# Linear-attention output gates: projected and applied in the gate stages instead of the GLA heads

## The chip, the cores and the metric

The kernel runs on one core of a Trainium2 chip. The metric is device time in microseconds (us), the median of several runs. The engines are TensorE (PE in the profile, with its weight loads as PEld), VectorE (DVE), ScalarE (ACT), GpSimd (POOL) and SyncE (SP), which here issues transfers only. ScalarE issues transfers as well, beside its own work.

## What is computed

One layer of a hybrid decoder over 2048 tokens of width 1024, with 16 extra tokens ahead. All is in float32. From u = RMSNorm(h), one combined projection gives the inputs of two branches (a Mamba-2 SSD branch and a gated linear attention branch, GLA) and the merge gates:

```python
z, xbc, dt_raw, q, k, v, g_gla, a_lr, merge_g = split_cols(proj, IN_WIDTHS)
...
o = rmsnorm(jnp.concatenate([o_m, o_r], axis=1), gla_norm_w)
y_gla = o.reshape(b, l, GLA_DV) * jax.nn.silu(g_gla)
branches = jnp.stack([y_ssd.astype(y_gla.dtype), y_gla], axis=2)
branch_proj = jnp.einsum('blnc,ncd->blnd', branches, w_branch)
gates = jax.nn.sigmoid(merge_g.reshape(b, l, N_BRANCH, D_MODEL))
merged = jnp.sum(gates * branch_proj, axis=2)
return hres + jnp.einsum('bld,de->ble', merged, w_out)
```

The change is about `g_gla`, the output gate of the linear attention (4 heads of 256 columns), and the product `o * silu(g_gla)`. The result then gets a last RMSNorm.

## The kernel before

**Precision.** Every large product is made of three matmuls: both factors are split into a high part (a rounded copy) and a low part (the rest), and high x high, high x low and low x high are summed (`accum`, L186 to L190). A split is one ScalarE copy and one VectorE or POOL subtraction.

**First stage.** Four blocks of 512 tokens (block 0 with the 16 extra tokens). In a block come 4 SSD units (`ssd_proj`) and 4 GLA heads (`gla_proj`, L625). A feature tile (`proj_feat`, L192) is a projection onto 128 columns: 8 x 3 = 24 matmuls of 512 columns, in two halves by weight transfer. A token-side projection (`proj_tok`, L204) of v is 96 matmuls of 256 columns. A GLA head projects q, k, v, and two feature tiles of the output gate; for each of these ScalarE makes tanh (L654) and VectorE (1 + tanh) times the value (L655), which is twice the silu. Weights are split in block 0, kept in memory (`k_...`), and reloaded by SP in blocks 1 to 3 (`load_w`, L164).

**Scans.** The recurrent part of a unit is a Python generator (`ssd_scan`, `gla_scan`), cut into segments by `yield`. `begin` starts one; each `yield` of a projection calls `step`, which runs one segment of every generator that is alive. So the segments stand between the projection's matmuls in TensorE's program, which is executed in the order written, as is SP's (`manual_schedule`). The order on VectorE, ScalarE and POOL is chosen by the scheduler when the kernel is built; each engine then works through its own list in order. A GLA scan has 11 segments: levels of the causal product (`level_in` on VectorE and ScalarE, L704 to L712; `level_out` on TensorE, L719), diagonal sums (L783), a merged matrix (L785 to L791), its transposes (L798), four chunks that accumulate output and state (L805 to L816: L809 on TensorE reads the state that L810 on VectorE writes for the chunk before), a normalization, transposes (L824), the gate's product on VectorE (L825), and the stores of y (L828). Beside these, `fetch_u` makes the next block's u (L248, L254), and `beside_unit` makes sums of u or y that the second stage needs (L80 on POOL).

**Second stage.** Gate stage, branch 0 and branch 1 for each of two superblocks of 1024 tokens, then the output stage (L1048). A stage is made of units. A unit takes 2 x 2 blocks of products (two feature tiles, two token blocks) in seven products instead of eight (Strassen's scheme in Winograd's form), 12 matmuls of 512 columns each, 84 in all, where single products would take 96. Units go in pairs. Each product is a step (`product`, L950); what else is issued at a step is set by a table of positions (`todo`, L1065): weight loads 7.5 steps ahead (`load_a`, four transfers and four POOL sums, L937 to L940), splits 5 steps ahead (`prep_a`, L946 and L947), the next stage's operand from 12 steps ahead (`prep_b`, L922 and L923). A gate stage has 8 units; `use` (L978) applies tanh to each of a unit's four results and stores it. Branch stages fetch these and p (L991) and multiply (L1002). Sums that are not ready in the first stage are made from `spots` (L1084).

## Time and profile before

| What | us |
| --- | --- |
| median of 3 runs | 2337.64 (2336.07 to 2343.33) |
| the profiled execution, whole | 2350.0 |
| its span from first to last instruction | 2348.2 |
| first stage with its last scan's end | 0 to 1554.4 |
| the GLA parts of blocks 0 to 3 in it | 196.4, 223.0, 226.7, 212.1 |
| second stage | 1554.4 to the end |

The profile lists busy times of each engine, groups of equal instructions by line and operands (count, busy time, mean duration, and the idle time just before them with what ended it), and single instructions in order of time. The durations of TensorE's instructions overlap, since they are pipelined, so their spacing or their busy time together is read, not one duration. "Idle before" is time in which that engine had nothing to run; on TensorE it is a wait that the kernel pays for, elsewhere it may cost nothing. The granted clock is the share of full speed that TensorE was given.

### The profile page before, as it was taken

Reading aid. Unit: us, or ns where it says so; the run is one execution under the profiler, and the core shown is the slowest. Engines: PE = TensorE matmul, PEld = TensorE weight load, DVE = VectorE, ACT = ScalarE, POOL = GpSimd, SP = SyncE. Lnnn points to the kernel's source line nnn. Section 1 sums busy time; section 2 is a strip of 40 time slices with the busy share of each in tenths; the row PEclk is TensorE's granted clock in tenths of the full one; section 3 lists DMA queues with packets and bytes.
Section 4 is the critical chain, followed back from the end, with each engine's and each line's share of the span. In section 5 each row is a group of like instructions: output and inputs, shape, how many; then the busy total and the mean of one; then the engine's idle time right before and its main releaser. Section 6 shows DMA issues by size and latency. Waiting matters only on the chain.

```text
span 2348.2 us, 36518 instructions
## 1 busy us (share of the span) xinstructions
PE 2253.1 (96%) x12651; PEld 1966.1 (84%) x12651; DVE 1566.5 (67%) x2884; ACT 1188.2 (51%) x2764; POOL 684.1 (29%) x677
## 2 busy tenths in 40 slices
PE   6899999999999999999999999889999999999998
PEld 6889989888888989798988898768788788777886
DVE  4676666676665667576568555674578864788876
ACT  5666655465534455543466443464555454544543
POOL 2344533122321212211122200207433355422441
PEclk9999999999999999999999999889999999999999
DMA  7665875767786666776676655447668866778762
GB/s 240 225 201 198 296 242 193 223 200 229 255 266 202 200 225 214 247 251 214 192 231 218 205 166 164 146 157 240 212 225 283 274 226 211 261 243 275 232 198 108
DMA packets 300937, 515.89 MB, mean 220 GB/s; under 512 B 27616, under 2 KB 143584, under 8 KB 300752
## 3 DMA queue, kind: packets, MB, share of 16 engines
q1 hardware_dynamic: 200080, 401.17, 52.9%
q10 hardware_dynamic: 100672, 112.39, 13.8%
q8 instruction: 99, 1.62, 0.3%
q14 instruction: 86, 0.70, 0.1%
HBM read 366.26 MB, written 147.19 MB: 219 GB/s over the span
## 4 chain that ended last, share of the span: by engine, by line
PE 39%; DMA 5%; DVE 4%; issue 2%; ACT 2%; SPq 0%; POOL 0%; ACTq 0%; DVEq 0%; POOLq 0%
PE psa L188 5%; PE psa L190 4%; PE psa L189 4%; PE pj L188 4%; PE pj L190 4%; PE pj L189 4%; PE psb L188 2%; PE psb L189 2%; PE psb L190 2%; DMA br<-br_t 2%; PE psc L188 1%; PE psc L189 1%; PE psc L190 1%; DMA br<-gate_t 1%; DVE b L923 1%
## 5 line engine op out<-in xcount | busy, mean ns | idle before, releaser
L188 PE MATMUL pj<-u,whl 128*128 128x512 f32 (+1 forms) x1184 | 450.6, 381 | 17.3 <-ACT acc L495 9.0
L190 PE MATMUL pj<-u,whl 128*128 128x512 f32 (+1 forms) x1184 | 433.9, 366 | 0.4 <-POOL whl L176 0.4
L189 PE MATMUL pj<-u,whl 128*128 128x512 f32 (+1 forms) x1184 | 433.5, 366 | 0.0
L188 PE MATMUL pj<-whl,u 128*128 128x256 f32 (+1 forms) x992 | 289.9, 292 | 2.7 <-ACT u L249 1.8
L190 PE MATMUL pj<-whl,u 128*128 128x256 f32 (+1 forms) x992 | 283.0, 285 | 3.9 <-DVE u L254 3.9
L189 PE MATMUL pj<-whl,u 128*128 128x256 f32 (+1 forms) x992 | 282.9, 285 | 0.7 <-POOL whl L176 0.7
L188 PEld LDWEIGHTS pj<-u,whl 128*128 128x128 f32 x1184 | 227.8, 192 | 56.7 <-ACT acc L495 10.0
L188 PE MATMUL psa<-b,a 128*128 128x512 f32 x640 | 253.1, 395 | 15.1 <-ACT sn L963 13.1
L190 PEld LDWEIGHTS pj<-u,whl 128*128 128x128 f32 x1184 | 227.0, 192 | 36.5 <-POOL whl L176 0.6
L189 PEld LDWEIGHTS pj<-u,whl 128*128 128x128 f32 x1184 | 227.9, 192 | 33.5
L190 PE MATMUL psa<-b,a 128*128 128x512 f32 x640 | 251.6, 393 | 0.0
L189 PE MATMUL psa<-b,a 128*128 128x512 f32 x640 | 251.5, 393 | 0.0
L947 DVE TENSOR_TENSOR a<-ar,a 128x512 fp32r<-128x512 f32 x160 | 151.6, 955 | 75.0 <-ACT a L946 73.2
L188 PEld LDWEIGHTS pj<-whl,u 128*128 128x128 f32 x992 | 190.5, 192 | 4.3 <-ACT u L249 1.9
L190 PEld LDWEIGHTS pj<-whl,u 128*128 128x128 f32 x992 | 190.4, 192 | 4.2 <-DVE u L254 4.2
L176 POOL TENSOR_TENSOR whl<-wr,whl 128x512 fp32r<-128x512 f32 (+1 forms) x100 | 135.3, 1360 | 199.3 <-ACT whl L175 155.8
L80 POOL TENSOR_TENSOR wr<-wr 128x256 f32<-128x256 f32 x80 | 66.9, 836 | 433.2 <-DMA wr<-y 178.2
L189 PEld LDWEIGHTS pj<-whl,u 128*128 128x128 f32 x992 | 190.5, 192 | 1.4 <-POOL whl L176 0.9
L923 DVE TENSOR_TENSOR b<-br,b 128x512 fp32r<-128x512 f32 x196 | 149.1, 783 | 48.4 <-ACT b L922 47.5
L937 POOL TENSOR_TENSOR as<-ar,ar 128x512 f32<-128x512 f32 x40 | 60.2, 1505 | 414.5 <-DMA ar<-in_w_br 107.8
L499 DVE SCALAR_TENSOR_TENSOR acc<-cin,hcw,acc 128x512 f32<-128x512 f32 (+1 forms) x192 | 154.8, 806 | 32.4 <-ACT acc L495 31.1
L922 ACT ACTIVATE b<-br 128x512 fp32r<-128x512 f32 x196 | 119.5, 626 | 95.7 <-DMA br<-br_t 36.6
(278 smaller groups left out, 5073.2 us busy)
## 6 DMA issues: line engine op xcount, KB each, us to landing
whl<-k_s SPq DMA_DIRECT2D x96, 512.0 KB, 4.2
whl<-k_g SPq DMA_DIRECT2D x96, 512.0 KB, 4.2
whl<-k_v SPq DMA_DIRECT2D x48, 512.0 KB, 3.8
whl<-k_z SPq DMA_DIRECT2D x36, 512.0 KB, 3.8
wr<-in_w_feat SPq DMA_DIRECT2D x64, 256.0 KB, 4.4
k_s<-whl SPq DMA_DIRECT2D x32, 512.0 KB, 3.9
cb<-cumd ACTq DMA_DIRECT2D x64, 256.0 KB, 5.6
y<-gg ACTq DMA_DIRECT2D x64, 256.0 KB, 4.4
```

What stands on the lines that cost most here:

```text
L80: nc.gpsimd.tensor_tensor(o, x, y, op=ALU.subtract)
L176: nc.gpsimd.tensor_tensor(hl[:, 1], raw, hl[:, 0].bitcast(F32), op=ALU.subtract)
L188: nc.tensor.matmul(ps, sh, mh, start=first, stop=False, **kw)
L189: nc.tensor.matmul(ps, sh, ml, start=False, stop=False, **kw)
L190: nc.tensor.matmul(ps, sl, mh, start=False, stop=last, **kw)
L499: nc.vector.scalar_tensor_tensor(acc, cin[:, k:k + tt], hcw[:, ti, k:k + 1], acc, op0=ALU.mult, op1=ALU.add)
L922: nc.scalar.activation(t[:, 0], raw, AF.Copy)
L923: nc.vector.tensor_tensor(t[:, 1], raw, t[:, 0].bitcast(F32), op=ALU.subtract)
L937: nc.gpsimd.tensor_tensor(s1, a21, a22, op=ALU.add)
L947: nc.vector.tensor_tensor(t[:, 1], src, t[:, 0].bitcast(F32), op=ALU.subtract)
```

## The change

The two gate tiles of each head leave `gla_proj`. A scan now stores the normalized y without its gate (L825 becomes a ScalarE activation, L826 of the changed file). A gate stage has 12 units instead of 8: the first eight alternate between a GLA head's gate and a merge gate. For a GLA unit it fetches y two products ahead, multiplies it with the projection, then with 1 + tanh, and stores the gated y under a new name (`yg`). Sums for branch 1 read `yg`, so those of the first superblock can't be made in block 2 any more: they move to the end of gate stage 0, and those of the second to the end of gate stage 1.

The projections of q, k and v of GLA heads yield at half pieces with a value of 0.5. `step` now counts: a generator of rate 1 runs a segment every two half steps, a GLA scan (rate 1.5) three in four; SSD units step as before. The scan begins before the last yield of v. Its old segments 10 and 11 are one. Buffers for y in the first stage (`gg`) go from 4 to 3.

```diff
-        yield from proj_tok(f"v{h}", w_tok[SG + h], o.u, o.starts + [0] * o.ci0, places)
+        yield from proj_tok(f"v{h}", w_tok[SG + h], o.u, o.starts + [0] * o.ci0, places, part=HALF)
...
-        yield
-        gs = []
-        for j in range(2):
-            ps, = proj_feat(f"g{t0 + 2 + j}", w_feat[t0 + 2 + j], o.segs_real, o.mov)
-            gg = mk(wk, [P, BLK], F32, "gg", bufs=4)
-            nc.scalar.activation(gg, ps, AF.Tanh, scale=0.5)
-            nc.vector.scalar_tensor_tensor(gg, gg, 1.0, ps, op0=ALU.add, op1=ALU.mult)
-            gs.append(gg)
-            yield
-        begin(gla_scan(o, h, qs, kf, (vh, vl), vm, gs))
+        begin(gla_scan(o, h, qs, kf, (vh, vl), vm), 1.5)
+        yield HALF
...
-            nc.vector.scalar_tensor_tensor(gs[j], ps, hgw[:, j:j + 1], gs[j], op0=ALU.mult, op1=ALU.mult)
-        yield
-        for j in range(2):
-            nc.scalar.dma_start(y_left[1][o.b][2 * h + j], gs[j])
+            yo = mk(wk, [P, BLK], F32, "gg", bufs=3)
+            nc.scalar.activation(yo, ps, AF.Identity, scale=hgw[:, j:j + 1])
+            nc.scalar.dma_start(y_left[1][o.b][2 * h + j], yo)
...
-    def begin(gen):
-        begun.append(gen)
-
-    def step():
+    def begin(gen, rate=1.0):
+        begun.append([gen, rate, 1 - rate * HALF if rate > 1 else 0.0])
+
+    def step(part=None):
         running.extend(begun)
         begun.clear()
-        for gen in list(running):
-            if next(gen, running) is running:
-                running.remove(gen)
+        for e in list(running):
+            e[2] = e[2] + part * e[1] if part else 1.0
+            if e[2] >= 1:
+                e[2] -= 1
+                if next(e[0], running) is running:
+                    running.remove(e)
...
+        def fetch(n, i, t):
+            if head(n) is not None:
+                got[n, i, t] = y = io()
+                nc.sync.dma_start(y, y_left[1][2 * s + t][2 * head(n) + i])
+
         def use(n, i, t, ps, snap):
             x = total(ps, snap)
+            if head(n) is not None:
+                y = got.pop((n, i, t))
+                nc.vector.tensor_tensor(y, y, x, op=ALU.mult)
             th = io() if snap is None else snap
             nc.scalar.activation(th, x, AF.Tanh, scale=0.5)
-            store(g_left[2 * s + t][2 * n + i], th)
+            if head(n) is not None:
+                nc.vector.scalar_tensor_tensor(y, th, 1.0, y, op0=ALU.add, op1=ALU.mult)
+                store(yg_left[2 * s + t][2 * head(n) + i], y)
+            else:
+                store(g_left[2 * s + t][2 * gate(n) + i], th)
...
-        return Stage(f"gate{s}", ("g", s), 8,
+        return Stage(f"gate{s}", ("g", s), 8 + GH,
...
-    spots = [g + 9 + 5 * k for g in begun_at for k in range(8)]
+            spots.append(begins[0] + 28 + 4 * k if key[1] == 0 else begins[3 * key[2]] + 62 + 4 * k)
```

Three places in the engines' lists. First TensorE in block 3, around the transposes L798 of that block's first scan. Before, they stand between the two gate tiles of the second head (L188 to L190 are the three matmuls of `accum`):

```order
L188 MATMUL pj_16029<-u_11309,whl_16044 128x512
L189 MATMUL pj_16029<-u_11309,whl_16044 128x512
L190 MATMUL pj_16029<-u_11309,whl_16044 128x512
L798 MATMUL pt_16061<-cst,sq_16022 128x128 x2
L188 MATMUL pj_16067<-u_11309,whl_16068 128x512
L189 MATMUL pj_16067<-u_11309,whl_16068 128x512
L190 MATMUL pj_16067<-u_11309,whl_16068 128x512
```

Now they stand inside the second half of the head's v, between its two banks (`accum` is L191 to L193 in the changed file):

```order
L191 MATMUL pj_14894<-whl_14975,u_10759 128x256
L192 MATMUL pj_14894<-whl_14975,u_10759 128x256
L193 MATMUL pj_14894<-whl_14975,u_10759 128x256
L798 MATMUL pt_15001<-cst,sq_14966 128x128 x2
L191 MATMUL pj_14895<-whl_14973,u_10759 128x256
L192 MATMUL pj_14895<-whl_14973,u_10759 128x256
L193 MATMUL pj_14895<-whl_14973,u_10759 128x256
```

The transposes moved from a place with 24 matmuls of 512 columns on either side to one with 24 of 256 columns on either side.

Second, VectorE's list in the same head, up to the first state update L810 of that scan. Before, it runs from the first gate tile's L655 (`sq` are levels of the next scan, `atp` the split of the merged matrix):

```order
L655 SCALAR_TENSOR_TENSOR gg_16058<-gg_16058,pj_16029 128x512
L709 TENSOR_TENSOR sq_16222<-sq_16221,act_15733 128x16x16
L704 TENSOR_TENSOR sq_16296<-g_all_13162 128x512
L237 TENSOR_TENSOR atp_16026<-pt_16061,atp_16025 128x2x128
L711 TENSOR_TENSOR sq_16222<-sq_16221,act_15673 128x2x4x16 x2
L709 TENSOR_TENSOR sq_16297<-sq_16296,act_15733 128x32x8
L711 TENSOR_TENSOR sq_16297<-sq_16296,act_15673 128x2x8x8 x2
L704 TENSOR_TENSOR sq_16308<-g_all_13162 128x512
L810 SCALAR_TENSOR_TENSOR s_gla<-s_gla,egl_15719,pc_16099 128x256
```

Now, with L244 for the low part of a split (`tok` from `pj` is v):

```order
L244 TENSOR_TENSOR tok_2604_14893<-pj_14894,tok_2603_14892 128x512
L244 TENSOR_TENSOR atp_14970<-pt_15001,atp_14969 128x2x128
L709 TENSOR_TENSOR sq_15163<-sq_15162,act_14786 128x8x32
L704 TENSOR_TENSOR sq_15174<-g_all_12318 128x512
L711 TENSOR_TENSOR sq_15163<-sq_15162,act_14691 128x2x2x32 x2
L244 TENSOR_TENSOR tok_2604_14893<-pj_14895,tok_2603_14892 128x512
L709 TENSOR_TENSOR sq_15175<-sq_15174,act_14786 128x16x16
L704 TENSOR_TENSOR sq_15209<-g_all_12318 128x512
L711 TENSOR_TENSOR sq_15175<-sq_15174,act_14691 128x2x4x16 x2
L810 SCALAR_TENSOR_TENSOR s_gla<-s_gla,egl_14677,pc_15052 128x256
```

The second v split, which needs the last matmul of v, and four level passes now stand between that matmul and L810, and TensorE's accumulations follow the same matmul. There are 12 such places, for the first three scans of each of the four blocks. In 3 of them the list reads so; in 5 the two L711 stand behind L810, and in 4 L810 follows the v split at once.

Third, VectorE in a gate stage. Before, in gate stage 1 (L947 are splits of weights, L974 adds two products):

```order
L947 TENSOR_TENSOR a_18235<-as_18027,a_18235 128x512
L974 TENSOR_TENSOR sn_18169<-sn_18169,psc_18201 128x512
L947 TENSOR_TENSOR a_18257<-as_18064,a_18257 128x512
L974 TENSOR_TENSOR sn_18190<-sn_18190,psc_18219 128x512
L947 TENSOR_TENSOR a_18276<-as_18029,a_18276 128x512
```

Now, in gate stage 0, in a pair of units with a GLA head (L949 and L976 are the same operations):

```order
L949 TENSOR_TENSOR a_17091<-as_16881,a_17091 128x512
L976 TENSOR_TENSOR sn_17019<-sn_17019,psc_17051 128x512
L949 TENSOR_TENSOR a_17111<-as_16918,a_17111 128x512
L997 TENSOR_TENSOR io_17022<-io_17022,sn_17019 128x512
L976 TENSOR_TENSOR sn_17046<-sn_17046,psc_17075 128x512
L1001 SCALAR_TENSOR_TENSOR io_17022<-sn_17019,io_17022 128x512
```

Two passes, L997 and L1001, came in for each result of a GLA head's unit.

55 lines of the change are left out of this document (36 added, 19 removed).

## The prediction

> **What bounds the kernel now.** I read the head of the page first, then the busy times of each stretch, then groups of instructions, then single waits.
>
> ```profile
> span 2348.2 us, 36518 instructions
> PE 2253.1 (96%) x12651; PEld 1966.1 (84%) x12651; DVE 1566.5 (67%) x2884; ACT 1188.2 (51%) x2764; POOL 684.1 (29%) x677
> ```
>
> TensorE is busy for 96% of the span, so time falls only where matmuls go away, and any wait that TensorE takes on is added in full. The next view cuts the span: the four GLA parts of the first stage (blocks 0 to 3), the drain of the last scan, and the second stage. Its columns are length, then busy time (and instructions) of PE, PEld, DVE, ACT, POOL, then granted clock and DMA.
>
> ```profile
> 227.60:424.00 196.40, 191.34 (x1261) 173.36 (x1260) 129.52 (x258) 106.46 (x274) 76.31 (x60) 0.99 0.70 241
> 566.00:789.00 223.00, 216.99 (x1314) 193.23 (x1313) 139.06 (x305) 100.68 (x267) 45.45 (x59) 0.98 0.71 229
> 929.50:1156.20 226.70, 218.22 (x1313) 194.62 (x1311) 139.09 (x305) 100.61 (x266) 44.80 (x60) 0.98 0.70 225
> 1297.00:1509.10 212.10, 212.06 (x1303) 189.98 (x1302) 119.33 (x272) 89.48 (x236) 22.45 (x27) 1.00 0.56 179
> 1509.10:1554.40 45.30, 27.48 (x117) 21.31 (x117) 33.59 (x69) 21.28 (x63) 10.37 (x8) 0.69 0.13 43
> 1554.40:2338.70 784.30, 771.05 (x3360) 634.16 (x3360) 567.63 (x770) 390.07 (x714) 299.81 (x230) 0.99 0.70 232
> ```
>
> In the GLA parts TensorE idles 5.1, 6.0, 8.5 and 0.0 us; in the drain 17.8; in the second stage 13.3 of 784.3. Everything but the drain is matmul-bound. VectorE has room in the GLA parts (56% to 66% busy), but it works in order, and its room shrinks with the matmuls that leave.
>
> **Part 1: the gate tiles leave the first stage.** The first two stretches are one gate tile each, 24 matmuls of 512 columns (rows of projections alone: PE, PEld, DVE, ACT, then clock and DMA). The third is gate stage 1 of the second stage, all engines. The fourth groups the first stage's 512-column matmuls: busy, mean ns, idle time before them.
>
> ```profile
> 1051.90:1057.50 5.60, 5.59 (x24) 4.42 (x24) 0.69 (x1) 0.58 (x1) 1.00 0.88 312
> 1058.60:1064.10 5.50, 5.48 (x24) 4.32 (x23) 0.67 (x1) 0.58 (x1) 1.00 0.87 281
> 1856.00:2011.00 155.00, 152.69 (x672) 126.03 (x672) 98.45 (x121) 76.73 (x135) 80.48 (x68) 1.00 0.69 228
> L188 PE MATMUL pj<-u,whl 128*128 128x512 f32 x864 | 352.2, 408 | 4.2 <-DMA whl<-k_g 4.2
> ```
>
> Two tiles for 4 heads in 4 blocks are 32 tiles, and at the mean of 5.55 us **177.6 us leave** TensorE. Their weight transfers go too (48 reloads of 512 KB in blocks 1 to 3, and block 0's 16 conversions with their stores). TensorE waited 4.2 us in all for weights like these (fourth row), so I give the lighter queue nothing, with 0 and -4.2 us as ends.
>
> **Part 2: they come back as units of seven products.** 4 heads in 2 superblocks are 8 units of 84 matmuls, 672 in all. The third row holds just that many of the same kind: **152.7 us come back.** The sum so far is -24.9 us: one product in eight (22.2) and some lead-in of the tiles.
>
> What lies beside them: each GLA gate adds two VectorE passes over 128x512 (y times x, then th plus one times y), 8 in a pair of units.
>
> ```profile
> 1775.00:1856.00 81.00, 80.14 (x353) 65.72 (x351) 71.06 (x95) 38.66 (x69) 26.44 (x17) 1.00 0.86 282
> L1002 DVE SCALAR_TENSOR_TENSOR io<-io,sn 128x512 f32<-128x512 f32 x48 | 44.8, 933 | 0.0
> L1006 DVE TENSOR_TENSOR io<-io,io 128x512 f32<-128x512 f32 x32 | 25.8, 806 | 0.4
> ```
>
> That is 4 x (0.81 + 0.93) = 7.0 us in a pair of units of 14 x 2.73 = 38 us, 18% of VectorE in a stage where 98.45 of 155 us (64%) were busy. The first row is a stage with VectorE at 88% that idles TensorE 0.9 us. So gate stages stay matmul-bound; I take +1 us, with 0 and +8 (one wait of a us in each of the 8 units) as ends. Loads of y are asked for two products (5.4 us) ahead; stores wait one product. The eight sums of branch 1 that move here (four subtractions on POOL each) find POOL at 52% of the third row's stage, and the last of them is stored nine products before the first is asked for; that covers them, and without it their subtractions (128x256) would stand ahead of branch stage 1 only. They leave block 2's GLA part, where POOL had twice the work of block 3.
>
> **Part 3: the scans beside shorter heads.** A head's projections were q, k, v (4 tiles' worth) and two gates. GLA scans advanced six segments in a head, and still do (eight half steps at rate 1.5: 8 x 0.5 x 1.5), but in a head shorter by 11.1 us, and a segment now follows 12 long or 24 short matmuls instead of 24 long or 48 short ones. Three places matter.
>
> First, the chain from the diagonal sums (L783) to the transposes (L798). The rows are VectorE's in one undisturbed head: start, duration, instruction.
>
> ```profile
> 1106.66 0.45 DVE L726 COPY_PREDICATED c<-msk,pc 128x256 f32<-128x256 uint8 x1 [3.95 <-PE pc L719]
> 1109.28 0.74 DVE L791 COPY_PREDICATED sq<-msk,pt 128x512 f32<-128x512 uint8 x1
> 1086.50:1092.10 5.60, 5.60 (x49) 5.60 (x48) 4.07 (x12) 2.81 (x10) 4.24 (x5) 1.00 0.36 119
> ```
>
> It takes 3.36 us, of which L655's 0.68 leaves with the gates: 2.7 us. It was covered by a 5.5 us tile; now by 24 matmuls of 256 columns, a quarter of v, at the third row's 0.114 us each 2.7 us, and what is left of L783. No wait while VectorE comes on time, but no slack either: nothing is taken here for undisturbed heads, 1 us in each of 16 if the split of v, which now stands in the same stretch, comes first.
>
> Second, the first two chunks' accumulations (L809) now follow the last v matmul directly, where VectorE first splits that v half.
>
> ```profile
> L236 ACT ACTIVATE tok<-pj 128x512 fp32r<-128x512 f32 x32 | 18.9, 591 | 29.9 <-PE pj L190 29.8
> L237 DVE TENSOR_TENSOR tok<-pj,tok 128x512 fp32r<-128x512 f32 x32 | 22.0, 687 | 19.9 <-ACT tok L236 19.8
> L709 DVE TENSOR_TENSOR sq<-sq,act 128x256 f32<-128x256 f32 x96 | 45.9, 478 | 6.7 <-PE pc L719 5.3
> L704 DVE TENSOR_TENSOR sq<-g_all 128x512 f32<-128x512 f32 x96 | 78.0, 813 | 0.5
> L711 DVE TENSOR_TENSOR sq<-sq,act 128x128 f32<-128x128 f32 x192 | 55.0, 326 | 0.0
> L810 DVE SCALAR_TENSOR_TENSOR s_gla<-s_gla,egl,pc 128x256 f32<-128x256 f32 x64 | 30.6, 478 | 72.3 <-PE pc L809 72.2
> 1070.69 0.28 PE L190 MATMUL pc<-tok,kdt 128*128 128x256 f32 x1
> 1075.44 0.64 PE L809 MATMUL pc<-s_gla,act 128*128 128x256 f32 x1 [2.97 <-DVE s_gla L810]
> ```
>
> By the changed order, from the last v matmul: 0.59 (ScalarE's copy), 0.69 (L237), then in 8 of 12 heads L709 and L704 (1.29), in 3 of them L711 twice (0.65) as well, then L810 (0.48): 3.05 or 3.70 us. TensorE reaches the second chunk's L809 after 2.0 us: the first of the last two rows is its third matmul, and the wait began at 1072.47. So waits of 1.05 us five times and 1.7 us three times: **+10.3 us**. In the other four heads L810 stands right behind L237, done after 1.8 us: none. Ends: 0 (ScalarE and VectorE ahead), and 12 x 3.7 = 44.
>
> Third, the heads where VectorE was late already, the first scan's in each of blocks 0 to 2, where the next block's u is made as well.
>
> ```profile
> 1064.70:1112.70 48.00, 45.03 (x267) 40.00 (x268) 29.68 (x66) 18.38 (x52) 8.81 (x11) 0.96 0.62 200
> 1422.60:1465.80 43.20, 43.20 (x268) 38.76 (x267) 23.12 (x58) 16.84 (x46) 2.19 (x1) 1.00 0.52 157
> L825 DVE SCALAR_TENSOR_TENSOR gg<-pt,hgw,gg 128x512 f32<-128x512 f32 x32 | 23.2, 746 | 16.8 <-PE pt L824 16.4
> L655 DVE SCALAR_TENSOR_TENSOR gg<-gg,pj 128x512 f32<-128x512 f32 x32 | 21.8, 680 | 7.8 <-ACT gg L654 7.8
> L597 DVE TENSOR_TENSOR tok<-c,tok 128x256 f32<-128x256 f32 x64 | 30.1, 470 | 1.2
> L248 DVE SCALAR_TENSOR_TENSOR acc<-acc,pv,cin 128x512 f32<-128x512 f32 x24 | 22.1, 924 | 17.9 <-DMA acc<-in_xmt 17.3 <-DVE gg L655 0.6
> 334.18 0.70 PE L809 MATMUL pc<-s_gla,act 128*128 128x256 f32 x2 [2.24 <-DVE s_gla L810]
> 700.50 0.48 PE L798 MATMUL pt<-cst,sq 128*128 128x128 f32 x1 [3.71 <-DVE sq L791]
> ```
>
> The first row is such a head, the second one of block 3, which had no wait. In the first, PE falls from 45.0 to 33.9 us. VectorE loses 2 x (0.75 + 0.68) = 2.9 and two passes of u (L248 and its split, 1.6 each, as u now advances four steps in a head, not six), and gains the ends of two SSD chunks (some five passes like L597 each, 4.7), since the SSD scan too has four steps: 29.7 - 2.9 - 3.2 + 4.7 = 28.3, **83% of what is left**. Block 3's head gets 23.1 - 2.9 = 20.2 in 32.1, 63%. At 83%, with L248's waits for its transfer in between, I expect 4 us of waits in each of three heads where 2.24, 3.71 (last two rows) and 2.97 stood: **+3 us** net. Ends: -9 (they vanish) and +20.
>
> The clock belongs to this; columns as in the second view, around the wait at 1075.44:
>
> ```profile
> 1072.50:1075.40 2.90, 0.00 (x0) 0.00 (x0) 2.72 (x9) 2.41 (x8) 0.00 (x0) 1.00 0.46 173
> 1075.40:1079.40 4.00, 3.96 (x10) 3.15 (x11) 1.68 (x3) 2.46 (x9) 0.00 (x0) 0.57 0.00 0
> 1079.40:1083.30 3.90, 3.90 (x19) 3.22 (x18) 0.00 (x0) 0.02 (x1) 0.00 (x0) 1.00 0.42 128
> ```
>
> After 2.9 us of idleness the granted clock was 0.57 for 4 us, so a wait of about 3 us costs 0.43 x 4 = 1.7 us more. The eight waits of 1.05 or 1.7 us are taken without it. The Trainium skill ("TensorE: Matmul & The Clock Gate", Part 1) has the clock halved after an idle window of about 3.4 us, in windows that run free of the kernel. The trace agrees in kind, with 2.9 us of idleness here. By that rule the sum stays as it is; by one in which any idleness halved the clock it would be 8 x 1.7 = 13.6 us higher.
>
> **Part 4: the drain.** At 1509 us the last scan but one still has its transposes and all four accumulations to do, and the last scan all of its segments. Now the former's transposes and the latter's first segment fall beside v. The stretch of 45.3 us has 27.5 of matmuls. I take **-5 us**; ends 0 and -12 (two thirds of its idle time).
>
> **Sum:** -177.6 + 152.7 + 1 + 10.3 + 3 - 5 = -15.6 us. Against the profiled execution (2350.0 us with a span of 2348.2) that is 2334.4; it lies 12.4 above the median of 2337.64, and the change is taken from the median: **2322 us**.
>
> **Rivals.** (A) The forecast: 2310 to 2331, a chance of 0.48. (B) No new wait forms, as ScalarE and VectorE run ahead, the old ones in blocks 0 to 2 go and the drain shortens: -24.9 - 9 - 5 + 1 = -38, 2300; for it speaks that block 3 had no wait at all with 60% VectorE; against, that the order puts VectorE's split behind the last v matmul. 0.15, for 2298 to 2310. (C) VectorE bounds the GLA heads: the three heads at 83% wait 8 us each, where 8.9 in all stood (+15), and the v waits are 1.7 us in all twelve (+20): -24.9 + 1 + 15 + 20 - 5 = +6, 2344; with three quarters of it 2335: no difference. For it speak the 2.97 and 3.71 us waits at 64% VectorE; against, that each is one of many heads. 0.22. (D) Slower: the wait for L810 is long everywhere. If VectorE reaches L237 2.0 us late in every head (at 1075.44 it was later than that), eight heads wait 3.05 or 3.7 us, 26.4 in all, four 1.8 us, 7.2 in all: -25.9 (all terms but that of the v waits) + 33.6 = +7.7. That is the point from which it decides; with the clock lowered after the eight long waits (13.6) it is +21, 2359. For it speaks that VectorE works in order; against, that without the first scan of a block its load is nearer to 63%. 0.15, for 2345 and above.
>
> **How the numbers follow.** A measurement of this kernel tells 0.3% (7 us) from no change. A and B are faster, C is no difference, D slower: 0.63, 0.22, 0.15. The range leaves out the lower part of B (0.05) and most of D (0.13): 2303 to 2348.
>
> **What would show it.** These are the waits of before that the change touches.
>
> ```profile
> L809 PE MATMUL pc<-s_gla,act 128*128 128x256 f32 x128 | 43.9, 426 | 6.0 <-DVE s_gla L810 5.7
> L798 PE MATMUL pt<-cst,sq 128*128 128x128 f32 x32 | 6.8, 297 | 5.8 <-DVE sq L791 5.8
> ```
>
> Right would be: projections shorter by 768 matmuls, the second stage longer by 672 and by 153 to 156 us; block 3's heads some 33 us apart and the first scans' 36 to 40; L809's wait near 16 us, in pieces of 1 to 2; L798's under 10; a drain near 40 us. The forecast is wrong if the gate stages' products no longer follow each other every 2.7 us, if the granted clock drops in block 3, or if TensorE waits for weights.

## The result, and the profile after the change

The change made the kernel slower: a median of 2369.88 us (2358.42 to 2374.20, 6 runs) against 2342.28 us (6 runs of the kernel before on the same chip), 27.6 us more by the medians; the ratio of the runs is 1.0097 with a 95% interval of 1.0074 to 1.0120, some 23 us. The forecast was 16 us faster. The profiled execution of the changed kernel took 2369.01 us.

Each kernel was traced a second time (runs before_again and a_again below). The parts of the four spans, in us:

| Part | before | again | after | again | change by the two pairs | forecast |
| --- | --- | --- | --- | --- | --- | --- |
| up to the first GLA head | 227.6 | 225.5 | 228.3 | 226.4 | +0.6, +0.9 | 0 |
| from there to the last projection | 1281.4 | 1274.4 | 1141.1 | 1138.2 | -140.3, -136.2 | -164.3 |
| drain | 45.3 | 45.0 | 41.5 | 40.7 | -3.8, -4.3 | -5 |
| second stage | 793.8 | 796.9 | 956.2 | 955.7 | +162.4, +158.8 | +153.7 |
| span | 2348.2 | 2341.8 | 2367.1 | 2361.1 | +18.9, +19.3 | -15.6 |

So 24 to 28 us are missing in the first stage and 5 to 9 in the second. The head of the page of the changed kernel:

```profile
span 2367.1 us, 36534 instructions
PE 2238.5 (95%) x12555; PEld 1953.7 (83%) x12555; DVE 1628.0 (69%) x2964; ACT 1243.2 (53%) x2860; POOL 734.4 (31%) x693
```

The same stretches as in the prediction's second view: the GLA parts of blocks 0 to 3, the drain, the second stage (length, then busy time and instructions of PE, PEld, DVE, ACT, POOL, then granted clock and DMA). In blocks 1 to 3 these stretches, before and after alike, begin with the z projection of the last SSD unit and not with the first GLA head.

```profile
228.25:393.28 165.03, 152.14 (x1086) 140.99 (x1085) 116.16 (x256) 97.59 (x262) 56.69 (x44) 0.98 0.61 210
537.24:729.19 191.95, 179.11 (x1136) 162.65 (x1135) 130.41 (x300) 100.63 (x269) 39.17 (x51) 0.96 0.65 213
870.10:1052.09 181.99, 174.66 (x1137) 158.44 (x1135) 125.95 (x300) 100.63 (x269) 19.05 (x27) 0.99 0.58 190
1193.66:1369.39 175.73, 169.65 (x1114) 154.32 (x1113) 112.77 (x262) 88.03 (x236) 25.77 (x28) 1.00 0.51 166
1369.39:1410.90 41.51, 25.81 (x115) 19.62 (x114) 27.91 (x63) 22.47 (x61) 6.12 (x6) 0.75 0.14 47
1410.90:2357.50 946.60, 926.65 (x4032) 762.49 (x4032) 688.50 (x914) 452.30 (x826) 387.94 (x294) 0.99 0.69 228
```

Eight gate tiles are 44.4 us of matmuls at the prediction's 5.55 us each. Block 2's part fell by 44.7 us (from 226.7), blocks 0, 1 and 3 by 31 to 36. TensorE idles 12.9, 12.8, 7.3 and 6.1 us there; it was 5.1, 6.0, 8.5 and 0. With the SSD parts between these stretches, its idle time from the first GLA head to the last projection is 48.9 us (49.6 in the second trace), and was 20.7 (20.9).

The waits by groups, of the kernel before (L584 is an SSD chunk's first product, L591 after the change):

```profile
L719 PE MATMUL pc<-sq 128*128 128x128 f32 x384 | 55.9, 282 | 2.6 <-DVE c L726 1.2 <-ACT junk L814 0.9 <-DVE s_gla L747 0.6
L584 PE MATMUL pc<-c,sq 128*128 128x64 f32 x512 | 65.5, 272 | 3.0 <-DVE sq L575 2.9
L188 PE MATMUL psa<-b,a 128*128 128x512 f32 x640 | 253.1, 395 | 15.1 <-ACT sn L963 13.1 <-ACT b L922 1.9
```

and of the changed one, with the two that the prediction named:

```profile
L719 PE MATMUL pc<-sq 128*128 128x128 f32 x384 | 58.6, 287 | 19.3 <-DVE c L602 7.8 <-DVE s_ssd L597 2.9 <-DVE s_gla L747 2.7
L591 PE MATMUL pc<-c,sq 128*128 128x64 f32 x512 | 66.1, 273 | 6.0 <-DVE sq L582 6.0
L809 PE MATMUL pc<-s_gla,act 128*128 128x256 f32 x128 | 43.7, 424 | 17.2 <-DVE s_gla L810 17.1
L798 PE MATMUL pt<-cst,sq 128*128 128x128 f32 x32 | 6.5, 287 | 2.6 <-DVE sq L791 1.9 <-ACT sq L708 0.7
L191 PE MATMUL psa<-b,a 128*128 128x512 f32 x768 | 303.9, 396 | 21.8 <-ACT sn L965 19.9 <-ACT b L924 1.9
```

L809 waits as forecast (17.2 us, 2.8 of it in the drain; "near 16"), L798 less. The largest new wait is one that the forecast doesn't have: L719, a level of the GLA scan, waits for L602 and L597, which belong to the **SSD** scan. One such place, TensorE first, then VectorE (start, duration, instruction, idle time before it):

```profile
963.80 1.00 PE L591 MATMUL pc<-c,sq 128*128 128x64 f32 x8
964.64 0.65 PE L592 MATMUL pc<-s_ssd,act 128*128 128x256 f32 x2
965.13 0.59 PE L594 MATMUL pc<-c,bt 128*128 128x256 f32 x2
966.82 0.68 PE L719 MATMUL pc<-sq 128*128 128x128 f32 x4 [1.09 <-DVE c L602]
```

```profile
965.33 0.42 DVE L599 TENSOR_TENSOR c<-pc,ecu 128x256 f32<-128x256 f32 x1 [0.79 <-PE pc L592]
965.67 0.67 DVE L764 TENSOR_TENSOR c<-g_all 128x128 f32<-128x128 f32 x2
966.26 0.41 DVE L602 TENSOR_TENSOR c<-c,pc 128x256 f32<-128x256 f32 x1
966.59 0.68 DVE L677 TENSOR_TENSOR act<-act,act 128x512 f32<-128x512 f32 x1
967.19 0.41 DVE L597 TENSOR_TENSOR s_ssd<-s_ssd,pc 128x256 f32<-128x256 f32 x1
```

The SSD chunk (L591, L592, L594) fills both banks of `pc`, the accumulators that the two scans share; the GLA segment of the same step stands right behind it and needs a bank. VectorE was idle before L599, so here it isn't late: the chain L599, L764, L602 is what TensorE waits for, and no projection stands between. A **joint step** is a step between two projections that holds both an SSD chunk and an L719: **there were none before and are nine after, with 10.7 us idle in them (11.1 in the second trace)**, three in block 0 and two in each later block. In three of the nine VectorE was idle before L599; in the other six it came to L599 0.5 to 1.4 us after the chunk's L592, since passes of levels or of u stood ahead. Before, an SSD scan ran six steps in a head, and its last chunk was done before the first GLA scan of the block had an L719. Now it runs four in a head, so its last two chunks (three in block 0) fall into steps of a GLA scan.

### The profile page after: what moved, and what is told of

Same layout as the page of the kernel before. It is cut to its first block, busy times and chain, and to the rows that moved or that the text cites. A ratio compares the mean times of both kernels' runs of the same rounds, so it can differ in the third digit from the quotient of the medians.

```text
span 2367.1 us, 36534 instructions
## 1 busy us (share of the span) xinstructions
PE 2238.5 (95%) x12555; PEld 1953.7 (83%) x12555; DVE 1628.0 (69%) x2964; ACT 1243.2 (53%) x2860; POOL 734.4 (31%) x693
## 4 chain that ended last, share of the span: by engine, by line
PE 42%; DMA 8%; DVE 5%; ACT 3%; issue 2%; SPq 1%; POOL 1%; ACTq 0%; DVEq 0%; POOLq 0%
PE psa L191 5%; PE psa L192 5%; PE psa L193 5%; PE pj L191 3%; PE pj L193 3%; PE pj L192 3%; PE psb L191 3%; PE psb L192 3%; PE psb L193 3%; DMA br<-gate_t 2%; DMA br<-br_t 1%; PE psc L192 1%; PE psc L191 1%; PE psc L193 1%; DMA io<-yg 1%
## 5 line engine op out<-in xcount | busy, mean ns | idle before, releaser
L191 PE MATMUL pj<-u,whl 128*128 128x512 f32 (+1 forms) x928 | 347.8, 375 | 20.2 <-ACT acc L502 13.1
L193 PE MATMUL pj<-u,whl 128*128 128x512 f32 (+1 forms) x928 | 332.2, 358 | 0.1
L192 PE MATMUL pj<-u,whl 128*128 128x512 f32 (+1 forms) x928 | 331.4, 357 | 0.0
L191 PE MATMUL psa<-b,a 128*128 128x512 f32 x768 | 303.9, 396 | 21.8 <-ACT sn L965 19.9
L192 PE MATMUL psa<-b,a 128*128 128x512 f32 x768 | 302.6, 394 | 0.0
L193 PE MATMUL psa<-b,a 128*128 128x512 f32 x768 | 302.3, 394 | 0.0
L191 PE MATMUL pj<-whl,u 128*128 128x256 f32 (+1 forms) x992 | 292.6, 295 | 2.7 <-ACT u L256 1.8
L193 PE MATMUL pj<-whl,u 128*128 128x256 f32 (+1 forms) x992 | 285.1, 287 | 3.8 <-DVE u L261 3.8
L949 DVE TENSOR_TENSOR a<-ar,a 128x512 fp32r<-128x512 f32 x192 | 185.6, 972 | 86.2 <-ACT a L948 85.2
L191 PEld LDWEIGHTS pj<-u,whl 128*128 128x128 f32 x928 | 178.3, 192 | 48.9 <-ACT acc L502 15.2
L939 POOL TENSOR_TENSOR as<-ar,ar 128x512 f32<-128x512 f32 x48 | 72.4, 1508 | 434.8 <-DMA ar<-in_w_feat 182.9
L193 PEld LDWEIGHTS pj<-u,whl 128*128 128x128 f32 x928 | 177.5, 191 | 25.5 <-POOL whl L179 0.4
L192 PEld LDWEIGHTS pj<-u,whl 128*128 128x128 f32 x928 | 178.5, 192 | 22.8
L191 PEld LDWEIGHTS pj<-whl,u 128*128 128x128 f32 x992 | 192.9, 194 | 4.5 <-ACT u L256 1.9
L193 PEld LDWEIGHTS pj<-whl,u 128*128 128x128 f32 x992 | 192.9, 194 | 4.2 <-DVE u L261 4.2
L192 PEld LDWEIGHTS pj<-whl,u 128*128 128x128 f32 x992 | 193.2, 195 | 2.3 <-POOL whl L179 1.2
L191 PEld LDWEIGHTS psa<-b,a 128*128 128x128 f32 x768 | 146.1, 190 | 57.2 <-ACT sn L965 24.7
L193 PEld LDWEIGHTS psa<-b,a 128*128 128x128 f32 x768 | 146.2, 190 | 30.9
```

Source lines behind the costliest of these rows:

```text
L191: nc.tensor.matmul(ps, sh, mh, start=first, stop=False, **kw)
L192: nc.tensor.matmul(ps, sh, ml, start=False, stop=False, **kw)
L193: nc.tensor.matmul(ps, sl, mh, start=False, stop=last, **kw)
L939: nc.gpsimd.tensor_tensor(s1, a21, a22, op=ALU.add)
L949: nc.vector.tensor_tensor(t[:, 1], src, t[:, 0].bitcast(F32), op=ALU.subtract)
```

## The experiments

Ratios are to the kernel before on the same chip, with the 95% interval. "Idle" is TensorE's from the first GLA head to the last projection; "joint" are the joint steps as just defined. Each trace is of one execution; some lie 3 to 9 us off the median of their runs, that of scans_together the most.

### A second trace of either kernel

> The kernel before once more, for a second trace of it. Its second stage lost 21.9 us beyond 280 products of 2.72 us; the four traces with the changed second stage lost 30.5 to 33.7. If that difference is the change's, this trace gives 20 to 24 again; if it is chance of one execution, 28 or more. TensorE's idle time from the first GLA head to the last projection should be within 2 us of the 20.7 of the first trace.

One run: 2343.6 us. The second stage lost 24.9 us beyond its products (24 at most was expected), idle time was 20.9.

> The changed kernel again, for a second trace of it. If the stages are set by fixed waits, the second stage begins within 4 us of 1410.9 and lasts within 4 us of 946.6 (784.2 before; 56 products more are 152.4). If the 10 us that the second stage took beyond its products are chance of that one execution, they come out differently here (between 0 and 15).

2362.96 us, 1.0087 [1.0058, 1.0116]. The second stage took 955.7 us and lost 31.3 us, 31.9 in the first trace. So both pairs of traces have the changed kernel lose 6 to 10 us more, though the waits fall on other changes of stages each time.

### The second stage: passes, sums, units, addresses

Without the gate's arithmetic (`use` stores tanh alone, nothing is fetched):

```diff
-                y = got.pop((n, i, t))
-                nc.vector.tensor_tensor(y, y, x, op=ALU.mult)
...
-                nc.vector.scalar_tensor_tensor(y, th, 1.0, y, op0=ALU.add, op1=ALU.mult)
-                store(yg_left[2 * s + t][2 * head(n) + i], y)
+                store(yg_left[2 * s + t][2 * head(n) + i], th)
```

> The changed kernel without the fetch of y and without the two VectorE passes of the gate stages: tanh of the gate alone is stored as the gated y, so the output gate is not applied. The forecast had 1 us for these passes and fetches: the second stage is 0 to 3 us shorter than 946.6. Theory G (they hold up VectorE and ScalarE in the gate stages, and the ends of those stages wait): the second stage is 6 to 12 us shorter, and the waits of L191 for ScalarE's L965 fall from 20 to about 12 us. The first stage is as in the changed kernel.

2362.1 us, 1.0075 [1.0052, 1.0097]; this kernel leaves out the output gate. Second stage 958.0 us. Its row up to the last product:

```profile
1405.12:2353.54 948.42, 927.19 (x4032) 762.38 (x4032) 632.32 (x850) 455.74 (x826) 377.64 (x294) 0.99 0.66 219
```

VectorE has 56 us less to do than in the last of the six rows above, and the stage isn't shorter but 1.8 us longer. So no cost of the passes can be seen (the forecast had 1 us), and theory G falls.

Branch 1's sums at their old places, from the ungated y:

```diff
-            beside[b, 0] = ("b", 0, s)
...
-        late.append(("b", 1, s))
+            beside.update({(b, 0): ("b", 0, s), (b, 4): ("b", 1, s)})
...
-        return lambda k, t: (yg_left if n else y_left[0])[2 * s + t][k]
+        return lambda k, t: y_left[n][2 * s + t][k]
```

> The changed kernel with branch 1's sums made where the kernel before made them (beside block 2's heads and early in gate stage 1), from the y without its gate, so the sums' operand lacks the gate; all products, gates and stores stay. Theory P (the sums, now made from the 62nd product of a gate stage on, when the next stage's operands are prepared, hold up that change of stages): the second stage is 6 to 10 us shorter than 956, and block 2's GLA part 4 to 8 us longer as it has POOL's work again. If the sums don't matter, the second stage stays within 3 us of 956.

2377.8 us, 1.0136 [1.0113, 1.0159]. The second stage took 958.4 us: theory P falls. Block 2's GLA part took 194.4 us instead of 182.0 (180.1 in the second trace), with 13.8 us of idle time instead of 7.3 and 7.4; the rest is mostly the clock, granted 0.96 instead of 0.99. In the next two kernels, which make these sums there too, it took 190.3 and 188.6 us. So moving the sums out of it was worth 7 to 14 us, which the forecast had as nothing.

Without the units as well (`gate_stage` as before the change, with the GLA gate left out):

> The changed kernel's first stage, with a second stage as before the change: no units for the GLA gates (they are left out, with their product), sums at the places of before from the ungated y. Second stage of before: 793.8 and 796.9 us, with 21.9 and 24.9 us beyond its products. If the 8 us that the changed second stage loses more belong to its 56 added products or what goes with them, 21 to 26 us here; if they come from elsewhere (the first stage's order, the place of y in memory), 29 to 35.

2217.9 us. The second stage, now with the 3360 matmuls of before, took 804.1 us and still lost 32.2. The units are not the cause either. What is left that differs are the first stage and the arrays' DRAM addresses: the first stage no longer keeps the gates' split weights, and so nearly all later arrays of this kernel lie 8 MB lower than before the change. With that space taken up again:

```diff
+            if b == 0:
+                for i in range(16):
+                    space = wdram.tile([P, 1024], F32, tag=f"space{i}", name=f"space{i}", bufs=1)
+                    nc.sync.dma_start(space[:, :4], mhalf)
```

> The kernel without the GLA gates' units (first stage as changed, second stage as before, the gate of GLA left out), with 8 MB of DRAM taken up after block 0, where the kernel before kept the split gate weights: the arrays of the second stage then lie where they lay before the change, all but a few. Without this they lay 8 MB lower, and the second stage lost 32.2 us beyond its products instead of 21.9 and 24.9. If their place in memory makes the difference, 21 to 26 us here; if not, 29 to 35.

2211.6 us; 801.4 us and 29.0 lost, the edge of "not". **This cause stays open.** In all the traces with the changed first stage the second lost 26 to 38 us beyond its products, before 21.9 and 24.9. TensorE's waits there are for ScalarE's copy L965, mostly around the changes of stages, 17 to 24 us in all (13.1 and 13.7 before).

### The steps of the first stage

Whole pieces instead of half ones, at the same number of segments in a head:

```diff
-                if part and i == 2:
-                    yield part
...
-            if e[2] >= 1:
+            while e[2] >= 1 and e in running:
```

> The changed kernel with the projections of q, k and v stepping whole pieces again (four steps in a head; a GLA scan runs 1, 2, 1, 2 segments there, an SSD scan 1 each): as many segments in a head as in the changed kernel, at coarser places. Theory H (the half pieces are too short a cover for the scans' chains): the first stage ends 15 to 25 us earlier than 1410.9, time about 2350. Theory L (VectorE has too little time in a head that is 11 us shorter, wherever the segments stand): no gain, and two segments in a row wait for each other, 5 to 30 us longer. Theory S (the SSD scans, now four steps in a head where there were six, run beside more of the GLA scans): no difference within 5 us.

2417.8 us, 1.0308 [1.0284, 1.0333]; idle 81 us. This is 55 us longer than the changed kernel, more than any of the three theories had. Half steps are not at fault. Two segments of one scan in a step wait for each other: L798 alone waits 31 us.

SSD scans at rate 1.5 (`begin(ssd_scan(o, g, feats, zs), 1.5)`):

> The changed kernel with the SSD scans begun at rate 1.5 as the GLA scans are: six SSD segments in a GLA head, as before the change. Theory S (SSD scans beside more GLA scans; both use the two banks pc, and L719 waits until VectorE has read the SSD chunk out of them): the waits of L719 for L602, L747 and L597, 14 us in all, fall below 5 and the first stage is 8 to 12 us shorter. Theories H and L: these waits stay or move to L591 and L809, and the first stage is within 5 us or longer, since VectorE gets the SSD work in a shorter time.

2359.4 us, 1.0068 [1.0047, 1.0090].

```profile
L591 PE MATMUL pc<-c,sq 128*128 128x64 f32 x512 | 65.5, 271 | 12.2 <-DVE sq L582 10.5 <-DVE c L602 1.7
L719 PE MATMUL pc<-sq 128*128 128x128 f32 x384 | 56.1, 281 | 5.3 <-DVE s_gla L747 1.9 <-DVE c L726 1.9 <-ACT junk L814 1.3
```

There are no joint steps, and L719's waits for L602 and L597 are gone: they come from the joint steps. But the SSD scan's own chain (VectorE's L582 before L591) has less time from step to step and waits 12.2 instead of 6.0 us; idle falls only from 48.9 to 46.5. Theory S was right on these waits and wrong on the 8 to 12 us.

GLA segments ahead of SSD segments in a step:

```diff
-        for e in list(running):
+        for e in sorted(running, key=lambda e: e[1] <= 1):
```

> The changed kernel with one line more: at a step the segments of GLA scans are issued ahead of those of SSD scans, where they followed them. All else is the same, VectorE's work too. Theory S (the two banks pc: L719 of a GLA segment comes right behind an SSD chunk that has just filled both, and waits until VectorE has read them): L719's waits for L602, L747 and L597 (14 us) fall below 5, TensorE's idle time from the first GLA head to the last projection from 49 to about 40, the time by 8 to 12 us. Theory L (VectorE is late in these heads, whatever stands where): the waits move to L591 or L809, idle time stays within 3 us of 49.

2372.8 us, 1.0126 [1.0109, 1.0142]; idle 54.1, joint steps 9 with 14.5 us. L719 no longer waits for L602, but 10.4 us for L711, the level's own operands, which VectorE now makes too late. Order within a step is no cure.

GLA scans a half step later (`begun.append([gen, rate, 0.0])`):

> The changed kernel with each GLA scan begun a half step later: its first two accumulations then stand behind the first half of the next head's q (12 matmuls of 512 columns) instead of right behind the last matmul of v. The forecast put 10.3 us on VectorE's split of v standing between that matmul and L810: L809's waits fall from 14.4 to 6 us or less and the time by 6 to 10 us. Theory L: they fall, but waits of L719, L798 or L591 come up elsewhere, and the sum of the idle time changes by less than 4 us.

2356.6 us, 1.0060 [1.0042, 1.0078]; idle 43.3, joint steps 5 with 5.4 us. In block 3's later heads, where nothing else runs, L809's 0.9 us are gone (32.4 and 32.2 us from v to v; 33.9 and 33.2 in the changed kernel). Elsewhere waits for L810 stay: 14.3 us in all. So the forecast's chain is real, but taking it away doesn't take away the waits.

SSD scans at odd half steps (a start value of 0.5 for them), alone, and with the shift:

> The changed kernel with the last SSD scan of each block stepping at odd half steps of the GLA heads instead of even ones (a start value of 0.5): an SSD chunk and a GLA segment then share two half steps in a head instead of four. Same work, same rates. Theory S (shared half steps, in which L719 waits until VectorE has read the SSD chunk out of the two banks pc): L719's waits for L602, L597 and L747 fall from 14 to about 7 us and the idle time from the first GLA head to the last projection from 49 to 42 or less; time 5 to 8 us shorter. If the shared half steps don't matter: these waits stay within 3 us of 14.

2361.1 us, 1.0063 [1.0047, 1.0080]; joint 4, but with 11.6 us in them, 1.5 to 4.1 us each; idle 45.6.

> As shift_half (GLA scans a half step later, 2356.5 us, idle 43.3, L719's waits for L602, L597 and L747 6.9 us), but with the SSD scans at odd half steps, so that SSD chunks and GLA segments share all four half steps again, as in the changed kernel. Theory S: L719's waits come back to 12 us or more and the time is 5 to 8 us longer than shift_half's. If shift_half's gain came from the accumulations L809 leaving the end of v, it stays: 2354 to 2359.

2350.1 us, 1.0014 [1.0003, 1.0025]; idle 35.9. This missed, and the test wasn't what I meant it to be: joint steps are 5, as in shift_half. They hold 12.0 us instead of 5.4, so what a joint step costs (1.0 to 2.9 us on average in these runs) isn't fixed; that it depends on what VectorE has ahead of the chunk was not tested by itself. L591's waits (7.2 us in shift_half) are gone, and the second stage of this one execution was 11 us shorter than shift_half's, though the two kernels have the same code there.

### How much there is to do, or where it stands

The matmuls of the gates put back, without any of their other work:

```diff
+            if pad is not None:
+                a, n = segs[-1]
+                for k4 in range(4):
+                    cs = slice(k4 * P, (k4 + 1) * P)
+                    accum(pad[:, :n], (h[:, cs], lo[:, cs]), moving(half * 4 + k4, a, n), k4 == 0, k4 == 3)
```

> The changed kernel with 12 matmuls of 512 columns added after each half of q and of k (48 in a head, as many as the two gate tiles had; their sums are overwritten or never read): the same segments at the same places, the same work on VectorE, ScalarE and POOL, but 11 us more of matmuls in a head. Theory L (a segment's chain through VectorE and ScalarE no longer fits into the matmuls between two steps): TensorE's idle time from the first GLA head to the last projection falls from 49 us to 25 or less, and the time is about 2365 + 178 - 24 to - 30 = 2513 to 2519. If the places of the segments are at fault (half steps, the split of v ahead of L810, the two banks pc), it stays above 40 and the time is 2535 or more.

2504.8 us; idle 33.4. (In block 0 the matmuls behind k are 264 wide, so 11 us less were added than the text says; with them the time would be 2516, as theory L had it.) The idle time lies between the theories:

```profile
L596 PE MATMUL pc<-c,sq 128*128 128x64 f32 x512 | 64.3, 269 | 0.4 <-DVE s_ssd L602 0.4
L726 PE MATMUL pc<-sq 128*128 128x128 f32 x384 | 57.0, 286 | 12.6 <-DVE s_ssd L602 5.3 <-DVE c L607 5.0 <-ACT junk L821 1.5
L816 PE MATMUL pc<-s_gla,act 128*128 128x256 f32 x128 | 43.0, 419 | 18.7 <-DVE s_gla L817 18.7
```

(The lines are five and seven numbers higher: L596, L602 and L607 are L591, L597 and L602, L726 and L816 are L719 and L809.) Waits across steps, as L591's, vanish with longer heads (6.0 to 0.4 us). Waits within a step stay: the nine joint steps hold 10.2 us (10.7), and L809 behind the split of v, where no matmuls were added, waits 18.7 us (17.2). No projection between the two can cover them.

The next block's u from the second head on (`if i == SG + 1 ...: begin(fetch_u(b + 1), 1.5)`):

> The changed kernel with the next block's u begun at the second GLA head of a block, at rate 1.5, instead of at the first: VectorE's passes for u leave the head in which the SSD scan still runs. Theory L (how much VectorE has to do in a head decides): from v to v, the first two heads of blocks 0, 1 and 2 stand 3 to 4 us closer (42 us in block 1 and 41 in block 2 become 38 and 37, as in block 3, where no u is made), the later heads 1 to 2 us farther apart; time 2358 to 2363. If the order within a head decides, not the amount: no change within 3 us in the first heads.

2375.4 us, 1.0126 [1.0104, 1.0149]; 41.9 and 42.1 us from v to v in the first heads of blocks 1 and 2, not 38 and 37. VectorE, then TensorE, in block 1's:

```profile
619.58 0.16 DVE L311 TENSOR_TENSOR ss<-ss 128x1 f32<-128x1 f32 x1 [3.43 <-ACT acc L310]
622.68 0.41 DVE L597 TENSOR_TENSOR s_ssd<-s_ssd,pc 128x256 f32<-128x256 f32 x1
623.14 1.22 PE L719 MATMUL pc<-sq 128*128 128x128 f32 x4 [3.91 <-DVE s_ssd L597]
```

A pass of 0.16 us at the head of VectorE's list waits 3.4 us for ScalarE, whose L310 waits for transfers of the next block's input, and the SSD chunk, the banks and TensorE wait behind it. VectorE had less to do in these heads and TensorE waited longer, 6.3 us in each instead of 4.3 and 4.5: the amount doesn't decide.

The gates of heads 0 and 1 kept in the first stage (their tiles beside q and k, 10 units in a gate stage):

> The changed kernel with the gates of heads 0 and 1 of each block kept in the first stage (12 of their matmuls behind each half of q and k, then tanh and products on ScalarE and VectorE as before the change), those of heads 2 and 3 in the gate stages: 16 tiles leave instead of 32, 4 units come instead of 8, -88.8 + 76.3 = -12.5 us of matmuls. Theory L with S (what was lost, was lost in the first two heads of each block, where the SSD scan runs beside a GLA scan in a head that is 11 us shorter): the first two heads of a block lose at most 2 us each, the time is 2335 to 2348. If the loss is spread over all heads alike: half of it remains, 2350 to 2356.

2368.5 us, 1.0108 [1.0093, 1.0123]. A miss: there are nine joint steps here as well, beside heads as long as before the change, and they hold 16.0 us.

### Towards a better version

POOL's sums out of block 1's heads:

```diff
-    beside = {(1, 0): ("o",), (1, 4): ("g", 0)}
-    late = []
+    beside = {(1, 0): ("g", 0)}
+    late = [("o",)]
```

> The changed kernel with only the sums moved: those for the output weights from block 1 into gate stage 1, those of u for gate stage 0 from block 1's GLA heads to its start, so that POOL has little to do in block 1's GLA heads. If POOL's work there held up VectorE: block 1's GLA part 4 to 8 us shorter (190 now, 182 in block 2), time 2357 to 2361. If not: within 3 us of the changed kernel.

2357.0 us, 1.0054 [1.0033, 1.0075]. Block 1's GLA part, POOL at 20 us instead of 39:

```profile
532.05:714.00 181.95, 174.43 (x1136) 158.44 (x1135) 125.94 (x300) 100.71 (x269) 20.21 (x27) 0.99 0.57 190
```

192.0 us (188.0 in the second trace) became 182.0, as long as block 2's. VectorE's same 300 instructions are busy for 125.9 us here and were for 130.4 in the second of the six rows above, and TensorE idles 7.5 us instead of 12.8 (11.9 in the second trace). With old_sums, this shows twice that POOL's sums beside GLA heads cost 6 to 14 us in a block.

> Three edits on the changed kernel at once: GLA scans a half step later (measured alone: 7 us), u from the second head on, and the sums that POOL made beside block 1's heads moved (those of the output weights into gate stage 1, those of u for gate stage 0 to the start of block 1). If they add up: 7 + 3 + 4 us less than the changed kernel, 2350, still above the kernel before (2343). If the second stage did not lose its 8 us it would be even with it. Below 2340 would mean that the waits had one common cause.

2341.8 us, 0.9989 [0.9973, 1.0006], 12 runs: no difference from the kernel before that can be measured; idle 33.5. Added up, the three edits would have given 2350.

> lighter_heads without its edit on u (which alone cost 11 us: its first steps put L311, which waits for a transfer, into VectorE's list ahead of the SSD chunk in the first head). If that edit cost as much there: 2330 to 2336, faster than the kernel before. If the gain of lighter_heads needed all three edits: 2348 to 2353.

2349.8 us, 1.0020 [1.0005, 1.0035], 12 runs. So u_late's edit, which cost 7 to 9 us alone (1.0126 against 1.0087 and 1.0097), gained 7 beside the other two, though in both comparisons the intervals lie close or overlap. Effects of moves don't add up here. No version beat the kernel before.

## Why the prediction was wrong

**The matmuls** were counted right, 768 away and 672 back, and +152.7 was right (56 products more at 2.72 us each are 152.3). -177.6 was 3.3 us too much: the rows of 5.6 and 5.5 us end with a tile's last matmul, whose end overlaps what follows. Its matmuls start 0.227 us apart, so 24 take 5.45 us and 32 tiles 174.3.

**Part 2, +1 us for the second stage**: nothing in the runs speaks against it for the passes (no_gate_math), the sums (old_sums) and the units (no_units); but the stage took 5 to 9 us more than forecast, for a cause that none of these four runs settled.

**The waits for L810, +10.3 us**: the mechanism was right where nothing else runs, the sum in part by luck. Here is a head of block 2, TensorE, then VectorE:

```profile
1050.57 0.28 PE L193 MATMUL pc<-tok,atp 128*128 128x256 f32 x1
1051.74 0.70 PE L809 MATMUL pc<-s_gla,act 128*128 128x256 f32 x2 [0.90 <-DVE s_gla L810]
```

```profile
1049.67 0.69 DVE L244 TENSOR_TENSOR tok<-pj,tok 128x512 fp32r<-128x512 f32 x1 [0.38 <-ACT tok L243]
1050.28 0.42 DVE L709 TENSOR_TENSOR sq<-sq,act 128x256 f32<-128x256 f32 x1
1050.61 0.68 DVE L704 TENSOR_TENSOR sq<-g_all 128x512 f32<-128x512 f32 x1
1051.21 0.48 DVE L810 SCALAR_TENSOR_TENSOR s_gla<-s_gla,egl,pc 128x256 f32<-128x256 f32 x1
```

Split, two passes, L810: 0.90 us of wait, 1.05 forecast. Three of the twelve places look like this. The others go both ways: where L810 follows the split at once, L809 waited 0.8 and 1.9 us in two of four places (none forecast); behind the longest list it waited 2.0, 0.7 and 0.0 (1.7 forecast), and once 2.7 where 1.05 was forecast. Eleven places came to 10.8 us, and the twelfth lies in the drain. All of L809's waits outside the drain came to 14.4 us, 16.3 forecast with those there before.

**The step that failed is the third place of part 3, "+3 us" for the heads in which the SSD scan and u run too.** The prediction saw that the SSD scan now has four steps in a head instead of six, and turned that into VectorE passes: 83% of a head, 4 us of waits in each of blocks 0 to 2 where 8.9 us stood before, none in block 3. The load was about right. These are blocks 1 to 3 from the end of the first v to the end of the second, beside which the first GLA scan runs (block 3 without u):

```profile
616.02:653.77 37.75, 35.62 (x230) 32.37 (x229) 32.66 (x79) 17.55 (x46) 6.82 (x8) 0.95 0.57 192
945.41:981.23 35.82, 34.06 (x230) 30.94 (x229) 31.34 (x79) 17.62 (x46) 3.07 (x4) 1.00 0.53 174
1265.55:1301.41 35.86, 33.21 (x222) 30.00 (x221) 27.82 (x74) 14.99 (x40) 2.95 (x4) 1.00 0.36 118
```

VectorE was busy for 87%, 87% and 78% of them. From the start of the first v to that of the second, blocks 1 to 3 took 42.6, 41.2 and 38.0 us (36 to 40 forecast), block 0 47.2.

What the prediction left out is which segments share a step. The idle time from the first GLA head to the last projection, 28.2 us more, is by steps: with matmuls of both scans 12.0 more (10.7 of it in the nine joint steps), SSD scan alone 3.5, GLA scan alone 10.5, the rest 2.2 in waits of the projections for ScalarE, POOL and weights. So where the SSD scan has a part it grew by 15.5 us, and the forecast had 3. Block 3, which makes no u and for which no wait was forecast, idles 4.5 us from its first v to its third; it was 0.0. Cover is not what was short in the joint steps: padded_qk, with 11 us more of matmuls in a head (less in block 0), left 10.2 us in them. ssd_rate_15 took the joint steps away, and L719's waits for the SSD scan with them, but L591's waits grew by 6.2 us; so no run won this time back by that alone.

The forecast's 10.3 stands against the 10.5 of the GLA scan alone, but 3.5 of these are another wait that it didn't have: L424, of the next block's decay factors, waits for L826, the ScalarE activation that took the place of VectorE's gate product and reads a bank of the pool that L424 writes to.

Of the busy time 168.5 us left, not 177.6: 3.3 us is the tiles' size as said above, 3.4 is the clock, whose halvings cost 13.7 us in these parts and 10.2 before, 1.7 is work that moved here from the drain, and under 1 is left. In the second pair of traces the halvings cost 10.2 us and 1.7, at the same idle times: this term differs from one execution to the next.

**Rivals.** C had VectorE's load as the cause and came to 2344; the load was there, but its 8 us in each of three heads and 1.7 us in all twelve places are not what the traces show. The time came out past D's 2359, though D's long wait for L810 everywhere did not happen: it was 0 to 2.7 us. **The drain** (41.5, "near 40"), block 3's later heads (33.9 and 33.2, "some 33"), L798 and the weights' waits (2.4 us) were as forecast. **The gain that the forecast had at nothing**: block 2's part became 44.7 us shorter, by its whole eight tiles, because POOL's sums left it.

## What to carry to other kernels

When generators (here the scans) are interleaved by steps, a new rate changes which segments stand back to back; count those pairs, in the order, for the banks they share. A wait between two segments of one step has no matmul to cover it, however long the steps are, and busy shares alone don't show it. Taking such pairs away can move the wait elsewhere, as ssd_rate_15 did. Sums on an idle engine beside a tight stage are not free: price them by moving them.

## What the runs showed of the hardware

The clock's drops don't follow the length of the idle time. Windows of the changed kernel, in and after a wait of 1.5 us, then in and after one of 2.7 us:

```profile
636.40:637.90 1.50, 0.04 (x1) 0.08 (x1) 1.50 (x6) 1.49 (x5) 0.63 (x1) 1.00 0.88 315
639.30:642.70 3.40, 3.40 (x18) 3.40 (x18) 3.40 (x11) 0.97 (x2) 0.00 (x0) 0.50 0.00 0
692.90:695.60 2.70, 0.00 (x0) 0.00 (x0) 2.70 (x6) 1.18 (x4) 0.18 (x1) 1.00 1.00 357
695.60:699.00 3.40, 3.39 (x15) 2.85 (x16) 2.69 (x8) 2.29 (x10) 0.00 (x0) 1.00 0.50 181
```

After 1.5 us of idleness the clock was halved for 3.4 us; after 2.7 us it was not. The prediction took waits of 1.05 and 1.7 us to be free of it. The seven drops between the first GLA head and the last projection of this trace begin whole multiples of 3.413 us apart (44.38, 194.56, 119.46, 34.14, 27.30 and 269.66 us, which are 13, 57, 35, 10, 8 and 79 times). That fits what the Trainium skill ("TensorE: Matmul & The Clock Gate", Part 1) says of windows that run free of the kernel, but not its idle window of about 3.4 us as the least that lowers the clock.

And the time up to the first GLA head, with the same 1442 matmuls in all kernels, lay between 223.0 and 230.0 us in these traces, with the clock halved for 10 to 20 us of it: a spread as large as most effects looked for here.
